# The y_gm projection of a hybrid decoder layer in seven block products

## The chip, the cores and the metric

One core of one Trainium2 chip runs the kernel. The metric is device time in microseconds (us), the median of several executions. TensorE multiplies matrices, VectorE and ScalarE work element by element, GpSimd fills masks and issues accumulating DMAs, and SyncE (SP) issues most of the loads.

## What is computed

One decoder layer on 512 positions and 1024 channels, in float32. A combined input projection feeds a gated MLP (y_gm) and an attention (y_nsa); both are projected, gated and added. The part that matters here:

```python
z = h @ w_in[l]
y_gm = spatial_gating(z_gm, ...)            # gelu(u) * (W_s LN(gelu(v)) + b), 512 x 1024
y_nsa = nsa_attention(z_q, k_cmp, v_cmp, z_ks, z_vs, z_kw, z_vw, sigmoid(z_g))
mix = (mg[:, :, 0] * (y_gm @ w_proj_gm[l]) + mg[:, :, 1] * (y_nsa @ w_proj_nsa[l])) @ w_out[l]
```

`w_proj_gm` is 1024 x 1024, so `y_gm @ w_proj_gm` multiplies a 512x1024 matrix by a 1024x1024 one. w_in, w_proj_nsa, w_out and the two feed-forward matrices (FF1, FF2) are the other large products.

## The kernel before, in words

**Precision.** Each float32 operand is split into a high part (a copy to float32r) and a low part (operand minus high part). A product takes three matmuls into the same PSUM bank: high x high, high x low, low x high (`mm3`, L132). `split` (L142) does this for weights: ScalarE writes `whi` (L150), VectorE subtracts to `wlo` (L151). Both have three buffers.

**The stream of weights.** `Stream` (L41) holds an ordered list of items. Each is one split, cut from a chunk that SP loads into a ring of buffers (L80); the ring `raw` has two buffers of 8 KB a partition. `ws.get()` hands out the next item and writes down the split of the item two places ahead, so that a split waits for the `whi` buffer of the product three before it. A chunk's next load waits for the last split that reads its buffer. The order of instructions on an engine is planned when the kernel is built and isn't always the written one, except under `manual_schedule`.

**The stages**, in the order of TensorE: u (L345 to 407); the v half of z_gm as seven block products (`products` L434, loop L464), with sums of weight blocks on VectorE in place (L223 to 229) in buffers of `rpool`, closed at L483; z_kc and z_vc (L524), each column tile by `dense_a` (L396): 8 steps of k, 3 matmuls of 512 columns each; the compression (L536), whose matmuls are 65 columns wide; z_ks and z_kw (L577), with the spatial gating `sg_mm` between them (L562); vs and vw (L595), whose weights are 256 and 280 columns and whose eight sums fill all eight PSUM banks; the projection of y_gm (L616); z_q (L624); then attention with z_m between its steps, the projection of y_nsa, w_out, FF1 and FF2.

**Around the change.** `sg_mm` writes uT (u times the gate, which is y^T) in eight tiles of 128 channels by 512 positions, and ScalarE and VectorE at once make ygh and ygl of them (L572, L575). After vs and vw the eight banks are emptied into V by ScalarE (L609) and VectorE (L612). The projection then takes for each of 8 tiles of 128 output channels a `whi`, `wlo` pair of 8x128 as stationary operand and ygh, ygl as the moving one, 24 matmuls of 512 columns, and ScalarE copies the bank to Y0 (L620). Its weights are four 1 MB chunks in ring `raw`, each cut into two items (`cols_a(w_pg, 0, 1024)`, L256). `bank()` (L121) takes PSUM banks in a fixed turn. `slab` (L113) takes one of eight 16 KB buffers.

The masks of the attention (Bm, Dc) are filled in `apool`, opened at L485, by GpSimd (L492 to 500), and scaled by ScalarE (L503). They are first read in the scores, after z_q.

The multiplication in seven products is in the kernel already, for v and for three quarters of FF2; there the stationary operand is the activation and the weights move, 512 columns at a time. Its order is `ORDER = (1, 2, 6, 5, 7, 3, 4)` (L177), and products add up in three banks in turn (A: 1, 6, 7, 4; B: 2; C: 5, 3), each emptied between two of them.

Of the kernel before, what the change touches and what calls it, by code (L numbers as in the profile page):

```python
# [16 lines left out]
P = 128  # L17
# [83 lines left out]
def layer_kernel(ctx: ExitStack, tc: tile.TileContext, x, w_in, gm_ln_g, gm_ln_b, gm_w_s, gm_b_s,  # L101
# [11 lines left out]
    def slab(name, shape, dt=F32):  # L113
        return slabs.tile(shape, dt, tag="slab", name=name)
# [39 lines left out]
    def add(shape, dmas, pieces, ring="raw"):  # L154
        c = ws.chunk(ring, shape, dmas)
        for view, dst in pieces:
            ws.item([c], lambda c=c, view=view, dst=dst: split(view(c["tile"]), dst))
# [76 lines left out]
    def s13(d):  # L234
        def go():
            for i in range(2):
                dma_add(d["S"]["tile"][:, i], d["U"]["tile"][:, i])
        return go

    add(**dict(shape=[1, 768], dmas=[(lambda t: t, wv[:, 0:1, 0:768])],  # L240
                       pieces=[((lambda t, j=j: t[:, 0, 384 * j:384 * j + 384]), None) for j in range(2)]))
    add(**dict(shape=[1, 768], dmas=[(lambda t: t, wv[:, 1:2, 0:768])],
# [7 lines left out]
    for k in range(0, 8, 2):  # L250
# [2 lines left out]
            dmas=[(lambda t: t[:, :, 0:256], wv[:, k:k + 2, C_VS:C_VS + 256]),  # L253
                  (lambda t: t[:, :, 256:536], wv[:, k:k + 2, C_VW:C_VW + 280])],
            pieces=[((lambda t, j=j: t[:, j]), None) for j in range(2)]))
    cols_a(w_pg, 0, 1024)  # L256
    cols_a(w_in, C_Q, 1024)
    cols_a(w_in, C_ZM, 2048)
    cols_a(w_pn, 0, 1024)
# [109 lines left out]
    def block(t, i):  # L369
        return t[:, i].rearrange("p (k t) -> p k t", k=4)  # L370
# [93 lines left out]
    for p in ORDER:  # L464
# [16 lines left out]
        if p == 7:  # L481
            cw_load(0, cmp_w1_k)
    early_pool.close()  # L483
    att = ctx.enter_context(ExitStack())
    apool = att.enter_context(tc.tile_pool(name="apool", bufs=1))  # L485
    Kh = apool.tile([P, 2, 1056], F32R, name="Kh")
    Kl = apool.tile([P, 2, 1056], F32R, name="Kl")
    Vch = apool.tile([32, 2, HD], F32R, name="Vch")
    Vcl = apool.tile([32, 2, HD], F32R, name="Vcl")
    Bm = apool.tile([P, 4, 512], F32, name="Bm")  # L490
    Dm = Bm[:, 0]
    nc.gpsimd.iota(Dm, pattern=[[-1, 512]], base=384, channel_multiplier=1,  # L492
                   allow_small_or_imprecise_dtypes=True)
    nc.gpsimd.affine_select(Dm, Dm, pattern=[[-1, 512]], compare_op=ALU.is_ge, fill=BIG,
                            base=384, channel_multiplier=1)
    Dc = apool.tile([P, 4, 32], F32, name="Dc")
    nc.gpsimd.iota(Dc, pattern=[[128, 4], [-16, 32]], base=-15, channel_multiplier=1,
                   allow_small_or_imprecise_dtypes=True)
    nc.vector.tensor_scalar(Dc, Dc, -0.5, None, op0=ALU.add)
    nc.gpsimd.affine_select(Dc, Dc, pattern=[[128, 4], [-16, 32]], compare_op=ALU.is_ge, fill=BIG,  # L500
                            base=-31, channel_multiplier=1)
    for i in (3, 2, 1, 0):
        nc.scalar.activation(Bm[:, i], Dm, AF.Copy, scale=2.0 ** -(i + 1))  # L503

    cw_load(1, cmp_w1_v)

# [49 lines left out]
        nc.vector.tensor_sub(Vcl, pv2, Vch.bitcast(F32))  # L556


    ygh = slab("ygh", [P, 8, S], F32R)
    ygl = slab("ygl", [P, 8, S], F32R)  # L560

    def sg_mm(g):  # L562
        ps = bank()
        for n in range(4):
            nc.tensor.matmul(ps[:, n * P:(n + 1) * P], v[:, n, g * P:(g + 1) * P], WsT[:, g],
                             start=True, stop=True)
        uv = uT[:, g].rearrange("p (n i) -> p n i", n=4)
        tmp = wpool.tile([P, 4, P], F32, tag="tmp", bufs=NTMP, name=f"sg{g}")
        nc.vector.tensor_tensor(tmp, ps.rearrange("p (n i) -> p n i", n=4),
                                bsb[:, g:g + 1].to_broadcast([P, 4, P]), op=ALU.add)  # L570
        nc.vector.tensor_mul(uv, uv, tmp)
        nc.scalar.activation(ygh[:, g], uT[:, g], AF.Copy)  # L572

    def sg_lo(g):
        nc.vector.tensor_sub(ygl[:, g], uT[:, g], ygh[:, g].bitcast(F32))  # L575

    for i in range(4):  # L577
        pc = ws.get()
        ps = bank()
        dense_a(ps, pc, xh, xl)  # L580
        ks = slice(32 + (i // 2) * S, 32 + (i // 2 + 1) * S)
        nc.scalar.activation(Kh[:, i % 2, ks], ps, AF.Copy)
        nc.vector.tensor_sub(Kl[:, i % 2, ks], ps, Kh[:, i % 2, ks].bitcast(F32))
        if i == 0:
            cmp_out()
        sg_mm(2 * i)
        sg_mm(2 * i + 1)
        sg_lo(2 * i)
        sg_lo(2 * i + 1)


    V = slab("V", [P, 2, 4, S], F32R)
    Vh, Vl = V[:, 0], V[:, 1]
    sb = [bank(t) for t in BANKS]
    for k in range(8):  # L595
        hi, lo = ws.get()
        for t in range(4):
            ts_ = slice(t * P, (t + 1) * P)
            for e in range(2):
                cs = slice(0, 256) if e == 0 else slice(256, 536)  # L600
                ps = sb[2 * t + e][:, 0:cs.stop - cs.start]
                nc.tensor.matmul(ps, xh[:, k, ts_], hi[:, cs], start=k == 0, stop=False)  # L602
                nc.tensor.matmul(ps, xl[:, k, ts_], hi[:, cs], start=False, stop=False)
                nc.tensor.matmul(ps, xh[:, k, ts_], lo[:, cs], start=False, stop=k == 7)  # L604
# [8 lines left out]


    Y0 = slab("Y0", [P, 8, S])
    for c in range(8):  # L616
        pc = ws.get()
        ps = bank()
        dense_a(ps, pc, ygh, ygl)
        nc.scalar.activation(Y0[:, c], ps, AF.Copy)  # L620
    nc.vector.tensor_scalar(E1, E1, 1.0, None, op0=ALU.add)
    Qh = slab("Qh", [P, 8, S], F32R)
    Ql = slab("Ql", [P, 8, S], F32R)
# [389 lines left out]
```

## Time and profile before

| | us |
|---|---|
| median of 3 runs | 891.54 (890.77 to 891.58) |
| profiled execution, its own time | 891.16 |
| span of the profiled execution | 889.4 |
| TensorE busy | 874.5 (98%) |
| VectorE, ScalarE, GpSimd busy | 529.6, 384.6, 24.3 |
| mean granted clock of TensorE | 0.997 |
| moved by DMA | 104.79 MB, 118 GB/s |

PE is TensorE's matmuls, PEld its weight loads, DVE is VectorE, ACT ScalarE, POOL GpSimd, SP SyncE. [...] `[x <-A]` behind a row says that the engine stood idle for x us and what released it. Some matmul records are missing from the trace.

### The profile page before, as it was taken

The numbers are of one execution on the slowest core, as the hardware profiler recorded it, in microseconds if no ns is written. First come the engines' busy times: TensorE is split into PE (matmuls) and PEld (weight loads), VectorE is DVE, ScalarE is ACT, GpSimd is POOL, SyncE is SP. The second block draws the span as 40 slices with busy tenths as digits, with TensorE's granted clock in tenths as the row PEclk, the third lists the DMA queues.
The fourth block names the chain that finished last, engine by engine and source line by source line (L and its number), as shares of the span: only waits on it lengthen the run. The fifth ranks groups of instructions, "written<-read, shape, count | busy, mean of one in ns | idle before, by whom it ended". The sixth has DMA issues, their size and how long they took to land.

```text
span 889.4 us, 11012 instructions
## 1 busy us (share of the span) xinstructions
PE 874.5 (98%) x4264; PEld 729.9 (82%) x4264; DVE 529.6 (60%) x1005; ACT 384.6 (43%) x668; POOL 24.3 (3%) x36
## 2 busy tenths in 40 slices
PE   8999999999999999999999999999999999999995
PEld 6888798988888888788878888888888888888884
DVE  3595935542236776666745588457457635853467
ACT  3555413242225656555633412563355345534500
POOL 0000000000000000000000000020011001100000
PEclk9999999999999999999999999999999999999998
DMA  6643810343321111121145441675566747541401
GB/s 200 221 154 95 250 59 25 95 145 95 95 94 49 48 48 48 53 91 48 48 143 188 142 142 48 189 166 173 181 158 127 237 139 168 129 133 47 142 24 71
DMA packets 70773, 104.79 MB, mean 118 GB/s; under 512 B 2432, under 2 KB 50368, under 8 KB 70720
## 3 DMA queue, kind: packets, MB, share of 16 engines
q1 hardware_dynamic: 62752, 83.99, 28.8%
q0 software_dynamic: 3456, 12.58, 7.5%
q10 hardware_dynamic: 4512, 7.50, 2.8%
q8 instruction: 33, 0.54, 0.2%
q14 instruction: 20, 0.16, 0.1%
HBM read 89.39 MB, written 2.10 MB: 103 GB/s over the span
## 4 chain that ended last, share of the span: by engine, by line
PE 96%; DVE 2%; DMA 1%; ACT 1%; issue 0%; SPq 0%; ACTq 0%; DVEq 0%
PE ps L133 19%; PE ps L134 19%; PE ps L135 19%; PE ps L451 5%; PE ps L449 5%; PE ps L452 5%; PE ps L819 3%; PE ps L817 3%; PE ps L818 3%; PE ps L744 2%; PE ps L539 2%; PE ps L759 1%; PE ps L761 1%; PE ps L760 1%; PE ps L602 1%; PE ps L604 1%
## 5 line engine op out<-in xcount | busy, mean ns | idle before, releaser
L151 DVE TENSOR_TENSOR wlo<-raw,whi 128x1024 fp32r<-128x1024 f32 (+3 forms) x116 | 134.0, 1162 | 157.4 <-ACT whi L150 154.0
L150 ACT ACTIVATE whi<-raw 128x1024 fp32r<-128x1024 f32 (+3 forms) x116 | 116.6, 1009 | 196.2 <-PE ps L134 142.7
L133 PE MATMUL ps<-xh,whi 128*128 128x512 f32 x320 | 129.7, 405 | 1.2 <-ACT whi L150 1.2
L134 PE MATMUL ps<-xl,whi 128*128 128x512 f32 x320 | 125.9, 394 | 0.0
L135 PE MATMUL ps<-xh,wlo 128*128 128x512 f32 x320 | 125.7, 393 | 0.0
L134 PE MATMUL ps<-hTl,whi 128*128 128x512 f32 x232 | 90.3, 389 | 0.0
L133 PE MATMUL ps<-hTh,whi 128*128 128x512 f32 x232 | 90.3, 389 | 0.0
L135 PE MATMUL ps<-hTh,wlo 128*128 128x512 f32 x232 | 90.3, 389 | 0.0
L135 PEld LDWEIGHTS ps<-xh,wlo 128*128 128x128 f32 x320 | 60.5, 189 | 13.1
L133 PEld LDWEIGHTS ps<-xh,whi 128*128 128x128 f32 x320 | 60.8, 190 | 11.5 <-ACT whi L150 2.0
L134 PEld LDWEIGHTS ps<-xl,whi 128*128 128x128 f32 x320 | 60.7, 190 | 9.9 <-DVE xl L343 0.4
L449 PE MATMUL ps<-whi,y 128*128 128x512 f32 x168 | 65.5, 390 | 0.0
L451 PE MATMUL ps<-whi,y 128*128 128x512 f32 x168 | 65.5, 390 | 0.0
L452 PE MATMUL ps<-wlo,y 128*128 128x512 f32 x168 | 65.5, 390 | 0.0
L703 ACT ACTIVATE PP<-PP,nm 128x512 f32<-128x512 f32 (+3 forms) x64 | 35.7, 559 | 35.6 <-DVE nm L697 35.3
L133 PEld LDWEIGHTS ps<-hTh,whi 128*128 128x128 f32 x232 | 43.6, 188 | 9.1
L135 PEld LDWEIGHTS ps<-hTh,wlo 128*128 128x128 f32 x232 | 43.6, 188 | 9.0
L134 PEld LDWEIGHTS ps<-hTl,whi 128*128 128x128 f32 x232 | 43.6, 188 | 8.9
L150 ACT ACTIVATE whi<-S 128x1024 fp32r<-128x1024 f32 x24 | 25.6, 1065 | 48.4 <-PE ps L451 35.3
L151 DVE TENSOR_TENSOR wlo<-S,whi 128x1024 fp32r<-128x1024 f32 x24 | 29.4, 1225 | 25.1 <-ACT whi L150 25.1
L909 DVE TENSOR_TENSOR y<-RR,y 128x512 fp32r<-128x512 f32 x50 | 33.1, 688 | 16.0 <-ACT y L908 16.0
L449 PEld LDWEIGHTS ps<-whi,y 128*128 128x128 f32 x168 | 31.5, 188 | 6.7
(235 smaller groups left out, 1712.6 us busy)
## 6 DMA issues: line engine op xcount, KB each, us to landing
raw<-in_w_in_dram SPq DMA_DIRECT2D x17, 1024.0 KB, 5.3
raw<-in_w_ff_dram SPq DMA_DIRECT2D x14, 1024.0 KB, 5.4
raw<-in_w_ff_dram SPq DMA_DIRECT2D x12, 512.0 KB, 4.2
S<-in_w_ff_dram SPq DMA_DIRECT2D x12, 512.0 KB, 4.1
S<-raw POOLq DMA_DIRECT2D x12, 512.0 KB, 6.7
S<-in_w_ff_dram SPq DMA_DIRECT2D x6, 1024.0 KB, 5.5
raw<-in_w_proj_gm_dram SPq DMA_DIRECT2D x4, 1024.0 KB, 5.0
raw<-in_w_proj_nsa_dram SPq DMA_DIRECT2D x4, 1024.0 KB, 4.9
```

The costliest lines, as they stand in the source:

```text
L133: nc.tensor.matmul(ps, hi, mh, start=start, stop=False)
L134: nc.tensor.matmul(ps, hi, ml, start=False, stop=False)
L135: nc.tensor.matmul(ps, lo, mh, start=False, stop=stop)
L150: nc.scalar.activation(hi, r, AF.Copy)
L151: nc.vector.tensor_sub(lo, r, hi.bitcast(F32))
L449: nc.tensor.matmul(ps, yh, hi[:, kk], start=opens and h == 0 and kk == 0, stop=False, skip_group_check=True)
L451: nc.tensor.matmul(ps, yl, hi[:, kk], start=False, stop=False, skip_group_check=True)
L452: nc.tensor.matmul(ps, yh, lo[:, kk], start=False, stop=h == 1 and kk == 1, skip_group_check=True)
L703: nc.scalar.activation(t, t, AF.Exp, bias=nm[:, e, i:i + 1], scale=-1.0, accum_out=sm[:, e, i:i + 1])
L817: nc.tensor.matmul(ps, th, hi[:, cs], start=start, stop=False)
L818: nc.tensor.matmul(ps, tl, hi[:, cs], start=False, stop=False)
L909: nc.vector.tensor_sub(Y[c][1][:, rows], t, Y[c][0][:, rows].bitcast(F32))
```

## The change

The projection of y_gm is done as two halves of the output channels (n = 0, 1). For each, the 1024x512 weights and the 1024x512 y^T are seen as 2x2 blocks, and seven products of sums of blocks take the place of eight. A block of weights is 512x256, one of y^T 512 channels by 256 positions. One product is one item of the stream: 2 tiles of output channels x 4 steps of k x 3 matmuls of 256 columns, with the weights stationary.

The weights of a half come as two chunks: two blocks in ring `raw`, two in a new ring `W` with one buffer in a new pool `mpool`. The sums are made by VectorE in place, but for one in a tile `s3`. The blocks of y^T take the place of ygh and ygl: eleven steps (seven splits, four sums in uT), two written down after each `ws.get()` of vs and vw, into slabs y12, y56, y37 and y4. A product's bank is copied to its quarter of Y0 by ScalarE (1, 6, 5, 4) or added to it or subtracted from it by VectorE (2, 3, 7). `mpool` closes after the projection, and `apool`, with the masks, opens only then; what was needed earlier of it (Kh, Kl, Vch, Vcl) moves to `kpool`.

```diff
@@ -237,6 +237,37 @@
                 dma_add(d["S"]["tile"][:, i], d["U"]["tile"][:, i])
         return go
+    ws.ring("W", 1, lambda shape, n: res["mpool"].tile([P] + shape, F32, tag="W", bufs=1, name=n),
+            ready=lambda: "mpool" in res)
+    def du_here(src, c0):
+        def blk(n, k):
+            return src[:, 4 * k:4 * k + 4, c0 + 256 * n:c0 + 256 * n + 256]
+        one, two = (lambda t: t[:, 0]), (lambda t: t[:, 1])
+        cu = ws.chunk("raw", [2, 4, 256], [(two, blk(0, 0)), (one, blk(1, 1))])
+        cw = ws.chunk("W", [2, 4, 256], [(one, blk(0, 1)), (two, blk(1, 0))])
+        d = {}
+        def item(p):
+            def make():
+                (a22, a11), (a12, a21) = (c["tile"].rearrange("p a k c -> a p k c") for c in (cu, cw))
+                out = split({1: a11, 2: a12, 6: a11, 5: a21, 7: d.get("s3"), 3: a12, 4: a22}[p])
+                if p == 1:
+                    d["s3"] = res["mpool"].tile([P, 4, 256], F32, tag="T", bufs=1, name=f"s3_{state['w']}")
+                    nc.vector.tensor_add(d["s3"], a21, a11)
+                    nc.vector.tensor_add(a21, a21, a22)
+                elif p == 2:
+                    nc.vector.tensor_add(a11, a11, a21)
+                elif p == 6:
+                    nc.vector.tensor_add(a12, a12, a11)
+                return out
+            ws.item([cu] if p in (4, 7) else [cu, cw], make)
+        for p in ORDER:
+            item(p)
     add(**dict(shape=[1, 768], dmas=[(lambda t: t, wv[:, 0:1, 0:768])],
                        pieces=[((lambda t, j=j: t[:, 0, 384 * j:384 * j + 384]), None) for j in range(2)]))
     add(**dict(shape=[1, 768], dmas=[(lambda t: t, wv[:, 1:2, 0:768])],
@@ -253,7 +284,9 @@
             dmas=[(lambda t: t[:, :, 0:256], wv[:, k:k + 2, C_VS:C_VS + 256]),
                   (lambda t: t[:, :, 256:536], wv[:, k:k + 2, C_VW:C_VW + 280])],
             pieces=[((lambda t, j=j: t[:, j]), None) for j in range(2)]))
-    cols_a(w_pg, 0, 1024)
+    pgv = w_pg.rearrange("(k p) c -> p k c", p=P)
+    for n in range(2):
+        du_here(pgv, 512 * n)
     cols_a(w_in, C_Q, 1024)
     cols_a(w_in, C_ZM, 2048)
     cols_a(w_pn, 0, 1024)
@@ -482,25 +515,13 @@
             cw_load(0, cmp_w1_k)
     early_pool.close()
     att = ctx.enter_context(ExitStack())
-    apool = att.enter_context(tc.tile_pool(name="apool", bufs=1))
-    Kh = apool.tile([P, 2, 1056], F32R, name="Kh")
-    Kl = apool.tile([P, 2, 1056], F32R, name="Kl")
-    Vch = apool.tile([32, 2, HD], F32R, name="Vch")
-    Vcl = apool.tile([32, 2, HD], F32R, name="Vcl")
-    Bm = apool.tile([P, 4, 512], F32, name="Bm")
-    Dm = Bm[:, 0]
-    nc.gpsimd.iota(Dm, pattern=[[-1, 512]], base=384, channel_multiplier=1,
-                   allow_small_or_imprecise_dtypes=True)
-    nc.gpsimd.affine_select(Dm, Dm, pattern=[[-1, 512]], compare_op=ALU.is_ge, fill=BIG,
-                            base=384, channel_multiplier=1)
-    Dc = apool.tile([P, 4, 32], F32, name="Dc")
-    nc.gpsimd.iota(Dc, pattern=[[128, 4], [-16, 32]], base=-15, channel_multiplier=1,
-                   allow_small_or_imprecise_dtypes=True)
-    nc.vector.tensor_scalar(Dc, Dc, -0.5, None, op0=ALU.add)
-    nc.gpsimd.affine_select(Dc, Dc, pattern=[[128, 4], [-16, 32]], compare_op=ALU.is_ge, fill=BIG,
-                            base=-31, channel_multiplier=1)
-    for i in (3, 2, 1, 0):
-        nc.scalar.activation(Bm[:, i], Dm, AF.Copy, scale=2.0 ** -(i + 1))
+    kpool = att.enter_context(tc.tile_pool(name="kpool", bufs=1))
+    Kh = kpool.tile([P, 2, 1056], F32R, name="Kh")
+    Kl = kpool.tile([P, 2, 1056], F32R, name="Kl")
+    Vch = kpool.tile([32, 2, HD], F32R, name="Vch")
+    Vcl = kpool.tile([32, 2, HD], F32R, name="Vcl")
+    mid = ctx.enter_context(ExitStack())
+    res["mpool"] = mid.enter_context(tc.tile_pool(name="mpool", bufs=1))
     cw_load(1, cmp_w1_v)
@@ -556,9 +577,6 @@
         nc.vector.tensor_sub(Vcl, pv2, Vch.bitcast(F32))
-    ygh = slab("ygh", [P, 8, S], F32R)
-    ygl = slab("ygl", [P, 8, S], F32R)
     def sg_mm(g):
         ps = bank()
         for n in range(4):
@@ -569,11 +587,6 @@
         nc.vector.tensor_tensor(tmp, ps.rearrange("p (n i) -> p n i", n=4),
                                 bsb[:, g:g + 1].to_broadcast([P, 4, P]), op=ALU.add)
         nc.vector.tensor_mul(uv, uv, tmp)
-        nc.scalar.activation(ygh[:, g], uT[:, g], AF.Copy)
-    def sg_lo(g):
-        nc.vector.tensor_sub(ygl[:, g], uT[:, g], ygh[:, g].bitcast(F32))
     for i in range(4):
         pc = ws.get()
         ps = bank()
@@ -585,15 +598,34 @@
             cmp_out()
         sg_mm(2 * i)
         sg_mm(2 * i + 1)
-        sg_lo(2 * i)
-        sg_lo(2 * i + 1)
     V = slab("V", [P, 2, 4, S], F32R)
     Vh, Vl = V[:, 0], V[:, 1]
+    y12 = slab("y12", [P, 4, D], F32R)
+    y56 = slab("y56", [P, 4, D], F32R)
+    y37 = slab("y37", [P, 4, D], F32R)
+    y4 = slab("y4", [P, 2, D], F32R)
+    Yg = {p: (block(t, i), block(t, i + 1)) for p, (t, i) in
+          {1: (y12, 0), 2: (y12, 2), 5: (y56, 0), 6: (y56, 2), 3: (y37, 0), 7: (y37, 2), 4: (y4, 0)}.items()}
+    b11, b12, b21, b22 = (uT[:, k:k + 4, c:c + 256] for k in (0, 4) for c in (0, 256))
+    def y_split(p, src):
+        nc.scalar.activation(Yg[p][0], src, AF.Copy)
+        nc.vector.tensor_sub(Yg[p][1], src, Yg[p][0].bitcast(F32))
+    steps = [lambda: y_split(1, b11), lambda: y_split(2, b21), lambda: nc.vector.tensor_sub(b11, b11, b12),
+             lambda: y_split(5, b11), lambda: nc.vector.tensor_sub(b12, b22, b12), lambda: y_split(3, b22),
+             lambda: nc.vector.scalar_tensor_tensor(b22, b11, -1.0, b22, op0=ALU.mult, op1=ALU.subtract),
+             lambda: y_split(6, b22), lambda: y_split(7, b12),
+             lambda: nc.vector.scalar_tensor_tensor(b21, b22, -1.0, b21, op0=ALU.mult, op1=ALU.subtract),
+             lambda: y_split(4, b21)]
     sb = [bank(t) for t in BANKS]
     for k in range(8):
         hi, lo = ws.get()
+        for _ in range(2):
+            if steps:
+                steps.pop(0)()
         for t in range(4):
             ts_ = slice(t * P, (t + 1) * P)
             for e in range(2):
@@ -613,11 +645,51 @@
     Y0 = slab("Y0", [P, 8, S])
-    for c in range(8):
-        pc = ws.get()
-        ps = bank()
-        dense_a(ps, pc, ygh, ygl)
-        nc.scalar.activation(Y0[:, c], ps, AF.Copy)
+    for n in range(2):
+        yg = {}
+        for p in ORDER:
+            where = {1: "A", 2: "B", 5: "C", 6: "A", 3: "C", 7: "A", 4: "A"}[p]
+            hi, lo = ws.get()
+            opens = p in (1, 2, 5)
+            if opens:
+                yg[where] = bank()
+            ps = yg[where]
+            for j in range(2):
+                js = slice(j * P, (j + 1) * P)
+                o = ps[:, j * 256:(j + 1) * 256]
+                for k in range(4):
+                    bh, bl = (b[:, k] for b in Yg[p])
+                    nc.tensor.matmul(o, hi[:, k, js], bh, start=opens and j == 0 and k == 0, stop=False,
+                                     skip_group_check=True)
+                    nc.tensor.matmul(o, hi[:, k, js], bl, start=False, stop=False, skip_group_check=True)
+                    nc.tensor.matmul(o, lo[:, k, js], bh, start=False, stop=j == 1 and k == 3,
+                                     skip_group_check=True)
+            c, h = {1: (0, 0), 2: (0, 0), 6: (0, 1), 5: (2, 1), 7: (2, 1), 3: (0, 1), 4: (2, 0)}[p]
+            y0 = Y0[:, 4 * n + c:4 * n + c + 2, 256 * h:256 * h + 256]
+            ps = ps.rearrange("p (k i) -> p k i", k=2)
+            if p in (1, 6):
+                nc.scalar.activation(y0, ps, AF.Copy)
+            elif p in (4, 5):
+                nc.scalar.activation(y0, ps, AF.Copy, scale=-1.0)
+            else:
+                nc.vector.tensor_tensor(y0, y0, ps, op=ALU.subtract if p == 7 else ALU.add)
+    mid.close()
+    apool = att.enter_context(tc.tile_pool(name="apool", bufs=1))
+    Bm = apool.tile([P, 4, 512], F32, name="Bm")
+    Dm = Bm[:, 0]
+    nc.gpsimd.iota(Dm, pattern=[[-1, 512]], base=384, channel_multiplier=1,
+                   allow_small_or_imprecise_dtypes=True)
+    nc.gpsimd.affine_select(Dm, Dm, pattern=[[-1, 512]], compare_op=ALU.is_ge, fill=BIG,
+                            base=384, channel_multiplier=1)
+    Dc = apool.tile([P, 4, 32], F32, name="Dc")
+    nc.gpsimd.iota(Dc, pattern=[[128, 4], [-16, 32]], base=-15, channel_multiplier=1,
+                   allow_small_or_imprecise_dtypes=True)
+    nc.vector.tensor_scalar(Dc, Dc, -0.5, None, op0=ALU.add)
+    nc.gpsimd.affine_select(Dc, Dc, pattern=[[128, 4], [-16, 32]], compare_op=ALU.is_ge, fill=BIG,
+                            base=-31, channel_multiplier=1)
+    for i in (3, 2, 1, 0):
+        nc.scalar.activation(Bm[:, i], Dm, AF.Copy, scale=2.0 ** -(i + 1))
     nc.vector.tensor_scalar(E1, E1, 1.0, None, op0=ALU.add)
     Qh = slab("Qh", [P, 8, S], F32R)
     Ql = slab("Ql", [P, 8, S], F32R)
```

## Rows read from the trace of the kernel before

**Rows 1.** the page: busy time and share by engine, and the chain by engine

```profile
PE 874.5 (98%) x4264; PEld 729.9 (82%) x4264; DVE 529.6 (60%) x1005; ACT 384.6 (43%) x668; POOL 24.3 (3%) x36
...
PE 96%; DVE 2%; DMA 1%; ACT 1%; issue 0%; SPq 0%; ACTq 0%; DVEq 0%
```

**Rows 2.** waits of PE, whole span: us in total, times, longest us

```profile
PE ps L133 <- ACT whi L150: 1.2, 2, 1.0
...
PE ps L602 <- DVE sg L569: 0.2, 1, 0.2
```

**Rows 3.** stretches: us, busy PE, PEld, DVE, ACT, POOL, PEclk, DMA share, GB/s

```profile
162.70:187.10 24.40, 24.22 (x195) 23.92 (x194) 10.48 (x15) 8.34 (x12) 0.00 (x0) 1.00 0.36 110
187.10:230.70 43.60, 43.60 (x195) 36.08 (x194) 12.34 (x16) 13.91 (x27) 0.00 (x0) 1.00 0.34 109
230.70:274.30 43.60, 43.60 (x194) 36.12 (x193) 14.01 (x15) 12.44 (x17) 0.00 (x0) 1.00 0.31 98
```

**Rows 4.** PE in order of time, projection of y_gm: start us, us, operation

```profile
187.13 0.40 PE L133 MATMUL ps<-ygh,whi 128*128 128x512 f32 x1
...
225.25 0.39 PE L133 MATMUL ps<-ygh,whi 128*128 128x512 f32 x1
...
230.69 0.39 PE L133 MATMUL ps<-xh,whi 128*128 128x512 f32 x1
```

**Rows 5.** PE in order of time, compression and FF1; loads of vs, vw

```profile
118.37 14.67 PE L539 MATMUL ps<-misc,cw 128*128 128x65 f32 x128
...
L604 PEld LDWEIGHTS ps<-wlo,xh x64: 187/188/192, 162.9 to 186.9; 128*128 128x128 f32 x64
...
556.16 0.28 PE L133 MATMUL ps<-hTh,e 128*128 128x256 f32 x1
...
558.50 0.28 PE L135 MATMUL ps<-hTh,e 128*128 128x256 f32 x1
```

**Rows 6.** groups by line and shape (busy us, mean ns); then VectorE in time

```profile
L151 DVE TENSOR_TENSOR wlo<-raw,whi 128x1024 fp32r<-128x1024 f32 x99 | 120.6, 1225 | 140.4 <-ACT whi L150 137.2 <-DMA raw<-in_w_ff_dram 3.2
L150 ACT ACTIVATE whi<-raw 128x1024 fp32r<-128x1024 f32 x99 | 104.5, 1059 | 179.8 <-PE ps L134 139.3 <-PE ps L451 14.4 <-PE ps L818 6.6
...
L575 DVE TENSOR_TENSOR ygl<-uT,ygh 128x512 fp32r<-128x512 f32 x8 | 5.5, 687 | 2.1 <-ACT ygh L572 2.1
...
L572 ACT ACTIVATE ygh<-uT 128x512 fp32r<-128x512 f32 x8 | 5.0, 631 | 13.6 <-DVE uT L571 13.6
...
L224 DVE TENSOR_TENSOR s<-s,raw x2: 1220/1220/1221, 44.8 to 53.9; 128x1024 f32<-128x1024 f32 x2
...
106.30 2.35 DVE L151 TENSOR_TENSOR wlo<-raw,whi 128x1024 fp32r<-128x1024 f32 x2
```

**Rows 7.** stretch in the v projection, columns as in rows 3

```profile
44.00:54.00 10.00, 10.00 (x46) 8.29 (x45) 10.00 (x10) 6.69 (x9) 0.00 (x0) 1.00 0.78 269
```

**Rows 8.** VectorE in order of time, last steps of uT and first V eviction

```profile
151.19 0.68 DVE L571 TENSOR_TENSOR uT<-uT,sg 128x512 f32<-128x512 f32 x1
...
166.03 0.69 DVE L571 TENSOR_TENSOR uT<-uT,sg 128x512 f32<-128x512 f32 x1
...
186.46 0.42 DVE L612 TENSOR_TENSOR V<-ps,V 128x256 fp32r<-128x256 f32 x1
```

**Rows 9.** VectorE in order of time, end of the v projection

```profile
85.70 0.29 DVE L517 COPY misc<-ps 128x32 f32<-128x32 f32 x2 [2.14 <-PE ps L516]
```

**Rows 10.** POOL, SP and PE in order of time, start of the z_kc projection

```profile
87.19 0.56 POOL L492 IOTA Bm<- 128x512 f32 x1 [28.75 <-DVE wlo L151]
...
89.63 1.50 SPq L80 DMA_DIRECT2D raw<-in_w_in_dram  x2
...
95.97 0.50 PE L133 MATMUL ps<-xh,whi 128*128 128x512 f32 x1 [0.99 <-ACT whi L150]
```

**Rows 11.** DMA issues: count, KB each, median us to landing; then SP's min/median/max

```profile
raw<-in_w_proj_gm_dram SPq DMA_DIRECT2D x4, 1024.0 KB, 5.0
...
DMA to landing us min/median/max: 2.7/5.0/10.9
```

## What the change is predicted to do

> **What bounds the kernel now.** I read the page first: TensorE is busy for 98% of the span, and the chain that ended last is 96% TensorE [rows 1]. The waits of TensorE come next: in the whole span it waits for about 5 us, of which the change can touch only 1.2 us at the start of the z_kc projection and 0.2 us at the start of vs and vw [rows 2]. So time is won here only by taking work from TensorE, and lost by anything that makes it wait. Then the stretches: vs and vw take 24.4 us and the projection of y_gm 43.6 us, both at a granted clock of 1.00, with VectorE busy for 10.5 and 12.3 us and ScalarE for 8.3 and 13.9 us of them [rows 3]. There is room beside TensorE, but in vs and vw the change fills it. Last, the matmuls in order of time. A row's duration (0.39 us) overlaps its neighbours, so I take the distance of starts: 225.25 to 230.69 holds the 24 matmuls of one column tile, 5.44 us, or 0.2267 us for 512 columns; the stage runs from 187.13 to 230.69, 43.56 us [rows 4].
>
> **TensorE's part.** Removed: 8 tiles x 8 k x 3 = 192 matmuls of 512 columns, 43.56 us. Added: 2 halves x 7 products x 2 x 4 x 3 = 336 of 256 columns. The same shape (weights stationary, 256 columns of activations moving) stands in the first FF1 tiles: 556.16 to 558.50 holds 20 starts, 0.117 us each [rows 5]. That is more than half of 0.2267, so seven eighths of the arithmetic isn't seven eighths of the time: 336 x 0.117 = 39.3 us. Bounds: 0.115 from the compression's matmuls of 65 columns, which I take as the floor for a weight load and its matmul (14.67 us / 128), gives 38.6; 0.127 from vs and vw (24.4 us / 192, half of them 280 columns wide and a small wait included) gives 42.7 [rows 3, 5]. I take 0.118, a little over FF1 for the 14 changes of product: 39.7 us, a gain of 3.9 (0.9 to 5.0). One product is then 24 x 0.118 = 2.8 us.
>
> [...] The row first: a weight load is recorded at 188 ns, and the change has 144 more of them [rows 5]. [...] By that measure the new stage would hold 336 x 188 ns = 63.2 us of loads. The trace disagrees with reading it as a limit: 192 loads at 188 ns, 36 us, fit in the 24.4 us of vs and vw. It is a rival below.
>
> **Splits and sums of the weights.** 8 splits become 14, with the same 128x1024 tiles: ScalarE 1.06 us and VectorE 1.23 us each, 1.14 back to back [rows 6]. Eight in-place sums on VectorE cost 1.22 us each, from the sums of the v projection [rows 6]. Eight evictions on ScalarE become eight there and six on VectorE, which at this width (128x512) cost 0.63 and 0.69 us [rows 6]. For one half: VectorE 7 x 1.14 + 4 x 1.14 + 3 x 0.69 = 14.6 us, ScalarE 7 x 1.06 + 4 x 0.63 = 9.9 us, under 7 x 2.8 = 19.7 us of TensorE. The v projection is the nearest case: half-products of 12 x 0.227 = 2.7 us with one split each and the same sums, VectorE busy for all of 44 to 54, and TensorE never stopped [rows 7]. I cost this at nothing as long as it runs in that rhythm: a split starts when the product three before it ends, since `whi` has three buffers, and has 5.6 us.
>
> **Blocks of y^T beside vs and vw.** Removed: eight ScalarE copies and eight VectorE subtractions of ygh and ygl (0.63 and 0.69 [rows 6]). Added: seven copies of 1.06 us, and seven subtractions and four sums, 11 x 1.14 = 12.5 us on VectorE. Its budget from 162.7 to 187.1 is 24.4 us. It now holds 10.5 [rows 3], less two ygl subtractions 1.3, plus 12.5, plus the first three sums of weights 3.4, makes 25.1: 0.7 too much. Three of the eleven steps (products 1 and 5) need only the upper half of uT, which is ready at 151.9, and could run earlier, which leaves 21.7. What waits for VectorE is the first product: its bank is free when the first V eviction has been read, and that ends at 186.88 now, 0.25 us before TensorE needs it at 187.13 [rows 8]. Bounds: everything placed in gaps, no stall; everything in written order, after the last step of uT (166.03 + 0.69 [rows 8], less the 0.6 of a ygl subtraction ahead of it, 166.1) the 11 steps and five splits of 0.65 us reach 181.8, with up to three waits of 1.06 us for ScalarE's copies 185.0, then two splits and three sums 5.7 us, then the eviction 0.42: 187.9 to 191.1, a stall of 0.8 to 4.0 us. Written order isn't kept strictly: the copy of L517, written after the v products, ran at 85.70, ten us before the matmul at 95.97 that follows them [rows 9, 10]. I take 0.6 us.
>
> **Loads.** The first load of ring W (1 MB) can start when the v projection's buffers are released, at 87.1, where GpSimd's iota of the same space starts now [rows 10]. The z_kc weights are issued at 89.63, and TensorE waits 0.99 us for their first split, until 95.97 [rows 10]. If W goes first on SP's queue, its 1 MB takes 5.0 us to land [rows 11], of which 2.5 are a head start: up to 2.5 us more wait; behind z_kc's, nothing. I take 0.1. The second load of W has one buffer to go to: it waits on SP for the split of product 3 of the first half; behind it stand z_q's loads, which wait for later splits anyway, and on VectorE the two sums of the second half wait for it. With the end of product 6 as zero, that split is done at 2.8, the load (5.0 us in the projection's rows [rows 11]) lands at about 8.0, the two sums end at 10.9 with an eviction among them, the split of the next product 2 at 12.4 at the latest, and TensorE wants it at 14.0; product 6 of the second half is ready at 15.9 of 16.8. Slack 0.9 us: I take 0.1, bounds 0 to 1. The two raw slots come free at the same splits of vs and vw as before, and the second chunk is now wanted 20 us later.
>
> **Bias masks.** Iotas, selects and four copies of 0.63 us leave the time from 87.19 on [rows 10] and go behind the projection, beside z_q, where ScalarE is busy for 12.4 of 43.6 us [rows 3]. The scores need them 40 us later. On GpSimd nothing is queued behind them; on ScalarE splits with over 5 us to spare are. Nothing, unless that cover went: then 2.5 us.
>
> **Sum.** -3.9 + 0.6 + 0.1 + 0.1 = -3.1 us against the profiled execution's 891.16 us (span 889.4): 888.1. The median, 891.54, lies 0.4 above that: 888.4.
>
> **Rivals.**
> 1. W's first load ahead of z_kc's. For: its space is free 2.5 us before theirs [rows 10]. Against: it is written later. 1 to 2.5 us: 889.3 to 890.8, taken as 890.0.
> 2. V's eviction held behind the y blocks, in written order. For: 25.1 us of work in 24.4. Against: rows 9. A stall of 2 to 4 us instead of 0.6: 889.8 to 891.8, taken as 891.
> 3. Slower: the sums of the second half are queued on VectorE ahead of product 4's split, and wait there for W's second load. The split then ends at landing + 3.5, and is wanted at 8.4. At 8.0 the stall is 3.1 and the gain is gone; slower by over 0.2% from a landing at 9.8 on, and the slowest load of the trace took 10.9 us where the middle one took 5.0 [rows 11]. A landing at 10.4, with a stall of 5.5, gives 893.9. Against: the split's inputs are there first.
> 4. Loads set the pace: 63.2 us instead of 39.7 gives 911; a pace of 43.56 / 336 = 0.1296 us gives no change, 891.5. Against: rows 5 for both.
>
> **How the numbers follow.** Forecast 0.65 (887.2 to 889.6), rival 1 0.11, rival 2 0.12, rival 3 0.06, rival 4 0.06 (0.01 of it at 911). A run of three tells about 0.2%, 1.8 us, from nothing: faster is under 889.76. Faster: 0.65 + 0.05 of rival 1 + 0.02 of rival 2 = 0.72. Slower: 0.05 of rival 3, 0.01 of rival 4 and 0.01 of rival 2 = 0.07. Same: 0.21. The range goes from 887.0 (0.117 and no stall would be 887.3) to 891.0, which leaves out half of rival 2, rivals 3 and 4 and a little of rival 1, 0.2 together.
>
> **What would show it.** TensorE's 336 starts 0.117 to 0.118 us apart, stage 39.7 us; VectorE nearly full from 163 to 187; a wait of TensorE for an eviction of V or a split at the first product; the wait before 95.97 unchanged; none in the middle. Wrong would be a distance over 0.12 us, a wait over 2 us at 187, or any repeated wait for `whi` or `wlo` in the products.

## Result: the products gained 3.2 us, and the start of z_kc lost more

| | before | after |
|---|---|---|
| median, us | 891.46 (890.77 to 891.58, 4 runs) | 897.30 (896.13 to 898.37, 4 runs) |
| profiled execution, its own time | 891.16 | 898.11 |
| its span | 889.4 | 896.4 |
| mean granted clock of TensorE | 0.997 | 0.990 |

After takes 1.0064 times as long as before (95% interval 1.0052 to 1.0076): 5.8 us slower by the medians (7.0 in the two profiled executions), where 888.4 was predicted and 891.0 was the upper end of the range.

The page of after, busy time by engine, the granted clock in 40 slices, and the chain (the lines of rows 1):

```profile
PE 873.7 (97%) x4408; PEld 735.8 (82%) x4408; DVE 557.7 (62%) x1028; ACT 392.6 (44%) x673; POOL 25.1 (3%) x36
PEclk9999799999999999999999999999999999999998
PE 96%; DVE 2%; DMA 1%; ACT 1%; issue 0%; SPq 0%; DVEq 0%; ACTq 0%
```

The chain is as before and says nothing. The clock line does: the fifth slice, 90 to 112 us, has a 7, a hundred microseconds ahead of the changed projection. The waits of TensorE in after, in us in total, times, and the longest (rows 2 before):

```profile
PE ps L135 <- DVE wlo L151: 6.4, 1, 6.4
PE ps L373 <- DMA xn<-in_x_dram: 2.4, 2, 2.1
PE ps L133 <- ACT whi L150: 2.1, 2, 1.9
```

The first line is new: one wait of 6.4 us for a low part of weights. The third was 1.2 in all [rows 2]. Neither the products (L662 to 665) nor the first V eviction has a line. TensorE in order of time in after shows where the wait is:

```profile
97.80 0.50 PE L133 MATMUL ps<-xh,whi 128*128 128x512 f32 x1 [1.91 <-ACT whi L150]
...
105.88 0.79 PE L135 MATMUL ps<-xh,wlo 128*128 128x512 f32 x1 [6.40 <-DVE wlo L151]
106.47 0.63 PE L133 MATMUL ps<-xh,whi 128*128 128x512 f32 x1
...
110.31 0.63 PE L133 MATMUL ps<-xh,whi 128*128 128x512 f32 x1
```

It is the start of z_kc, the place of rival 1. From 106.47 to 110.31 the starts are 0.427 us apart (nine steps), where a matmul of 512 columns took 0.2267 [rows 4]. The wait, the stretch behind it and the two stages around the change as windows of after (us, busy PE, PEld, DVE, ACT, POOL, granted clock, DMA share, GB/s; rows 3 before):

```profile
97.80:105.88 8.08, 1.47 (x4) 0.60 (x5) 7.73 (x18) 1.96 (x2) 0.00 (x0) 0.68 1.00 279
105.88:110.70 4.82, 4.82 (x11) 3.80 (x12) 4.82 (x6) 0.00 (x0) 0.00 (x0) 0.50 0.52 158
173.50:197.50 24.00, 24.00 (x195) 23.90 (x195) 21.92 (x25) 11.93 (x15) 0.00 (x0) 1.00 0.35 112
197.50:237.80 40.30, 40.30 (x338) 40.30 (x337) 29.54 (x34) 22.20 (x36) 1.65 (x4) 1.00 0.25 79
```

The granted clock is 0.50 from 105.88 to 110.70, after a stretch in which TensorE had run four matmuls in 8 us. The mean of 0.68 over that stretch says that it fell during the wait already: it is 1.00 from 97.80 to 99.50, 0.88 from 99.50 to 101.00 and 0.50 from there to 105.88. In the two stages of the change it is 1.00.

Now the time by starts of stages, before to after, from the matmuls in order of time:

| | before | after | shift |
|---|---|---|---|
| first matmul of z_kc | 95.97 [rows 10] | 97.80 | +1.8 |
| first matmul of the compression | 118.37 [rows 5] | 129.22 | +10.8 |
| first matmul of the projection of y_gm | 187.13 [rows 4] | 197.53 | +10.4 |
| first matmul of z_q | 230.69 [rows 4] | 237.85 | +7.2 |
| end of the span | 889.4 | 896.4 | +7.0 |

Of the +1.8, 0.9 is the longer wait for `whi` (1.91 for 0.99), and most of the rest is the wait for `xn` at the very start (2.4 here, 1.6 in before), which the change doesn't touch. Between z_kc and the compression 9.0 are lost: 6.4 are the wait, 2.4 the half clock behind it (ten starts 0.427 apart instead of 0.227, and one at each end that is longer by 0.4 together), and 0.2 come in because the wait is counted from the end of the last matmul's record, 0.40 us behind its start, where the next could have started 0.227 behind it. From the compression to the projection after is 0.4 shorter, of which 0.2 is the wait for `sg` that is gone [rows 2]. The projection gives 3.2 back, 40.32 us for 43.56.

Who kept the low part? SP of after in order of time (start us, us, operation):

```profile
88.05 0.92 SPq L80 DMA_DIRECT2D W<-in_w_proj_gm_dram  x2
90.38 16.98 SPq L80 DMA_DIRECT2D raw<-in_w_in_dram  x3
```

ScalarE of after in order of time:

```profile
96.69 2.00 ACT L150 ACTIVATE whi<-raw 128x1024 fp32r<-128x1024 f32 x2 [0.28 <-ACT v L508]
```

VectorE of after in order of time:

```profile
97.25 0.21 DVE L549 BATCH_NORM_AGGREGATE mv<-st 128x2 f32<-128x12 f32 x1
...
99.75 1.54 DVE L529 TENSOR_SCALAR v<-v,mv,rs 128x1024 f32<-128x1024 f32 x2
101.20 2.35 DVE L531 TENSOR_TENSOR v<-v,gmc 128x1024 f32<-128x1024 f32 x2
103.47 1.22 DVE L532 TENSOR_TENSOR v<-v,gmc 128x1024 f32<-128x1024 f32 x1
104.61 3.49 DVE L151 TENSOR_TENSOR wlo<-raw,whi 128x1024 fp32r<-128x1024 f32 x3
```

The high part that `wlo` needs was written from 96.69 on and took about 1 us. VectorE didn't stand idle: from 97.25 it ran the end of v's layer norm (aggregate, twelve small steps of the reciprocal root, five steps that normalise v), and only at 104.61 the three subtractions of z_kc, back to back. In before the order was the other way round. VectorE of before:

```profile
95.95 2.36 DVE L151 TENSOR_TENSOR wlo<-raw,whi 128x1024 fp32r<-128x1024 f32 x2 [0.24 <-ACT whi L150]
...
101.45 1.53 DVE L508 TENSOR_SCALAR v<-v,mv,rs 128x1024 f32<-128x1024 f32 x2
```

Nothing of the layer norm was edited. The diff moves two things near this place: the first load of ring W, now on SP ahead of z_kc's weights (88.05 and 90.38), and the masks, which left it. `wlo` had its operands for over 6 us and still ran behind the normalisation. That VectorE ran the order of the built program there is argued from this, not shown by the trace; e2 below, where the program ties the layer norm behind z_kc's first splits, has the first two of them at 96.58.

### The profile page after: what moved, and what is told of

Read it like the earlier page. It is cut to its first block, busy times and chain, and to the rows that moved or that the text cites. A ratio compares the mean times of both kernels' runs of the same rounds, so it can differ in the third digit from the quotient of the medians.

```text
span 896.4 us, 11356 instructions
## 1 busy us (share of the span) xinstructions
PE 873.7 (97%) x4408; PEld 735.8 (82%) x4408; DVE 557.7 (62%) x1028; ACT 392.6 (44%) x673; POOL 25.1 (3%) x36
## 4 chain that ended last, share of the span: by engine, by line
PE 96%; DVE 2%; DMA 1%; ACT 1%; issue 0%; SPq 0%; DVEq 0%; ACTq 0%
PE ps L133 18%; PE ps L135 18%; PE ps L134 18%; PE ps L484 6%; PE ps L482 6%; PE ps L485 6%; PE ps L891 3%; PE ps L889 3%; PE ps L890 3%; PE ps L816 2%; PE ps L560 2%; PE ps L665 1%; PE ps L662 1%; PE ps L664 1%; PE ps L831 1%; PE ps L833 1%
## 5 line engine op out<-in xcount | busy, mean ns | idle before, releaser
L151 DVE TENSOR_TENSOR wlo<-raw,whi 128x1024 fp32r<-128x1024 f32 (+3 forms) x114 | 131.4, 1159 | 130.0 <-ACT whi L150 129.8
L150 ACT ACTIVATE whi<-raw 128x1024 fp32r<-128x1024 f32 (+3 forms) x114 | 114.4, 1008 | 190.9 <-PE ps L134 136.2
L485 PEld LDWEIGHTS ps<-wlo,y 128*128 128x128 f32 x168 | 31.5, 188 | 6.7
```

Source lines behind the costliest of these rows:

```text
L150: nc.scalar.activation(hi, r, AF.Copy)
L151: nc.vector.tensor_sub(lo, r, hi.bitcast(F32))
L485: nc.tensor.matmul(ps, yh, lo[:, kk], start=False, stop=h == 1 and kk == 1, skip_group_check=True)
```

## The experiments

Theory A: W's load, put ahead of z_kc's, delays these a little, and the order planned with that delay in it puts the layer norm of v ahead of z_kc's splits on VectorE; that order and the half clock behind it cost most, the load itself about 1 us. Theory B: the load itself, 1 MB ahead of z_kc's on the DMA engines, costs it all. Theory C: the masks that left the place changed the order. (Each expectation below states its own theories by letter; what it calls B isn't always this B.) In the edits, `tc.issue_after(x)` puts what stands in its block behind instruction x on its engine.

**e1_load_behind: W's first load behind z_kc's on SP.**

```diff
                 for dv, src in c["dmas"]:
-                    self.nc.sync.dma_start(dv(c["tile"]), src)
+                    with self.behind() if c["ring"] == "W" and c["n"] == 0 else ExitStack():
+                        i = self.nc.sync.dma_start(dv(c["tile"]), src)
+                if c["ring"] == "raw":
+                    self.last_raw = i
...
+    ws.behind = lambda: tc.issue_after(ws.last_raw.ins)
```

> The changed kernel, with the first load of ring W queued on SP behind the second load of the z_kc weights; nothing else is edited, and VectorE's planned order at the start of z_kc is then again that of the kernel before. Theory A (the load in front delays the z_kc weights, and the plan made with that delay puts the normalisation of v ahead of their splits on VectorE): the wait of 6.4 us and the half clock go, the wait before z_kc is 1 us again, and the gain of the products remains: 887.5 to 888.5 us. Theory B (the seven products and the y blocks cost the time somewhere else, and the stall at z_kc only moves it): 893 us or more.

Measured: 887.69 us (886.24 to 888.62), 0.9958 of before (0.9943 to 0.9973). SP of e1 in order of time:

```profile
91.23 9.02 SPq L81 DMA_DIRECT2D raw<-in_w_in_dram  x3
100.35 4.94 SPq L81 DMA_DIRECT2D W<-in_w_proj_gm_dram  x2
...
199.28 0.92 SPq L81 DMA_DIRECT2D W<-in_w_proj_gm_dram  x2
```

VectorE of e1 in order of time:

```profile
97.50 2.36 DVE L155 TENSOR_TENSOR wlo<-raw,whi 128x1024 fp32r<-128x1024 f32 x2
```

TensorE of e1 in order of time, first matmuls of z_kc, of the projection and of z_q:

```profile
97.52 0.50 PE L136 MATMUL ps<-xh,whi 128*128 128x512 f32 x1 [0.78 <-ACT whi L154]
...
188.22 0.28 PE L666 MATMUL ps<-y,whi 128*128 128x256 f32 x1
...
228.53 0.40 PE L136 MATMUL ps<-xh,whi 128*128 128x512 f32 x1
```

With the load behind, the first two splits are ahead of the layer norm again, the 6.4 us wait is gone, and the change is worth 3.8 us where 3.1 were predicted, at 887.69 for 888.4. The projection takes 228.53 - 188.22 = 40.31 us. This kernel is faster than before (by 0.4%) and than after. C falls: the masks have moved here too.

**e2_dve_order: W's load left in front, the layer norm put behind z_kc's first splits.**

```diff
-            for t in range(4):
-                nc.vector.bn_aggr(mv[:, t], st6[:, t])
-            rstd(mv[:, :, 1], EPS, 0, 4)
+            with tc.issue_after(los[-2].ins):
+                for t in range(4):
+                    nc.vector.bn_aggr(mv[:, t], st6[:, t])
+                rstd(mv[:, :, 1], EPS, 0, 4)
```

> The changed kernel with the first load of ring W still in front of the z_kc weights, but with the statistics and the normalisation of v tied on VectorE behind the splits of the first z_kc chunk. Theory A (most of the loss is VectorE's order, 6.4 us of wait and about 2.6 us of half clock, the late load itself only some 1 us): 888 to 890 us, with a wait of about 2 us left before the first z_kc matmul. Theory B (the load itself holds TensorE up, whatever VectorE's order): the stall stays near 6 us and the time near 897 us.

Measured: 889.63 us (888.50 to 891.28), 0.9983 of before (0.9973 to 0.9992). The waits of TensorE in e2:

```profile
PE ps L133 <- ACT whi L152: 1.9, 1, 1.9
...
PE ps L135 <- DVE wlo L153: 0.5, 1, 0.5
```

VectorE of e2 in order of time:

```profile
96.58 2.36 DVE L153 TENSOR_TENSOR wlo<-raw,whi 128x1024 fp32r<-128x1024 f32 x2 [0.56 <-ACT whi L152]
```

A window of e2 over the place (columns as above):

```profile
94.00:112.00 18.00, 15.56 (x68) 12.34 (x67) 16.63 (x31) 6.76 (x9) 0.00 (x0) 1.00 0.98 293
```

The load is still 2.3 us ahead of z_kc's on SP (86.85 and 89.17), and 7.7 of after's 897.30 us are gone. The wait for `whi` is the same 1.9 us, the one for `wlo` is 0.5, and the clock stays at 1.00. B falls: in front, the load costs about 889.63 - 887.69 = 1.9 us, as rival 1 had it (1 to 2.5), and the order on VectorE the rest. The 1.9 is not the load's alone, since e2 also puts z_kc's third split ahead of the layer norm, which before and e1 don't.

**e3_load_only and e4_masks_only: before, with one part of the change each.** e4 takes before's masks to the place after the projection, Kh, Kl, Vch and Vcl to `kpool`. e3 does that and adds the load, into a buffer that nothing reads:

```diff
+    ws.ring("W", 1, lambda shape, n: res["mpool"].tile([P] + shape, F32, tag="W", bufs=1, name=n),
+            ready=lambda: "mpool" in res)
+    ws.chunk("W", [2, 4, 256], [((lambda t: t[:, 0]), pgv[:, 0:4, 256:512]), ((lambda t: t[:, 1]), pgv[:, 4:8, 0:256])])
```

> The kernel before with its eight tiles of y_gm, with the masks moved behind the projection and with the first load of ring W added, which nothing reads. Theory A: the same stall at z_kc as in the changed kernel without the products' gain of 3.2 us: 900 to 901.5 us. Rival (the products, the sums or the y blocks are needed for the loss): 891 to 893 us.

> The kernel before with the masks moved behind the projection of y_gm and the small pool for K and V opened in their place; no load is added. Theory A: VectorE's order at z_kc is as before, no stall: 891 to 892 us. Rival (the moved masks change the order there): 897 us or more.

Measured: e3 901.72 us (901.22 to 902.57), 1.0119 of before (1.0102 to 1.0136); e4 890.82 (890.20 to 891.63), 0.9992 (0.9983 to 1.0002). TensorE's wait in e3:

```profile
PE ps L135 <- DVE wlo L151: 6.9, 1, 6.9
```

z_kc's splits on VectorE of e3:

```profile
104.50 3.49 DVE L151 TENSOR_TENSOR wlo<-raw,whi 128x1024 fp32r<-128x1024 f32 x3
```

And in e4:

```profile
PE ps L133 <- ACT whi L150: 1.4, 2, 1.1
```

A load that nothing reads makes the kernel of before 10.2 us slower (901.72 against 891.49 for before, measured beside it), with the wait of after and the splits at 104.50 as in after; the masks alone change nothing that can be told. Two DMA instructions on SP are enough for the whole loss. That the planner moved the layer norm because it counted with later weights is argued from this, not shown: its reckoning isn't in a trace.

**e5_second_load_late: the second load of W a product later (from here on all kernels are e1 with an edit).**

```diff
-            ws.item([cu] if p in (4, 7) else [cu, cw], make)
+            ws.item([cu] if p == 7 else [cu, cw], make)
```

> As e1_load_behind (887.69 us), but product 4 of the first half also holds ring W's chunk, so the second load of W can start only behind product 4's split instead of product 3's, one product (24 x 0.120 = 2.9 us) later. The result is computed in full. Theory as in the prediction (the second load has 0.9 us of slack before VectorE's sums hold up the products): the first wait of TensorE appears in the second half, about 2 us, and the time is about 889.7. Rival (the slack is larger than computed, because the load or the sums come sooner than the working has them): no wait of TensorE in the products, 887.7 within 0.6.

Measured: 887.73 us (887.37 to 888.76). This is the rival's time, but it tells nothing of the slack, because the edit didn't move the load. VectorE of e5, the split of product 3 in the first half:

```profile
196.69 1.23 DVE L155 TENSOR_TENSOR wlo<-W,whi 128x1024 fp32r<-128x1024 f32 x1 [1.65 <-ACT whi L154]
```

SP of e5, the second load of W:

```profile
197.94 0.92 SPq L81 DMA_DIRECT2D W<-in_w_proj_gm_dram  x2
```

The load goes out 1.25 us after the split of product 3 begins, when that has been read. e9 does what e5 was to do.

**e9_second_load_behind: the second load behind z_q's first on SP.** As e5, and:

```diff
-                    with self.behind() if c["ring"] == "W" and c["n"] == 0 else ExitStack():
+                    with self.behind() if c["ring"] == "W" else ExitStack():
```

> As e1_load_behind, but the second load of W stands on SP behind the first load of z_q, which waits for the split of product 4 of the first half: so it is issued one product (2.9 us) later and shares the DMA engines with another 1 MB. (e5_second_load_late was meant to do that, but its load was still issued right behind product 3's split, 1.25 us after that split began, as in e1_load_behind.) The result is computed in full. Theory (about 1 us of slack, as in the prediction; in e1_load_behind the split of product 2 ends 1.0 us before its product is due): the delay of 3 to 5 us leaves a wait of TensorE of 2 to 4 us at product 2 or 6 of the second half, and some half clock behind it, 890 to 893 us. Rival (the order on VectorE gives way and hides it): a wait under 0.5 us, 887.7 to 888.3.

Measured: 893.29 us (891.21 to 894.79), 1.0019 of before (1.0009 to 1.0029): 5.6 us more than e1. TensorE of e9 in order of time, from the first matmul of the projection to the first of z_q:

```profile
187.59 0.28 PE L666 MATMUL ps<-y,whi 128*128 128x256 f32 x1
...
211.41 0.39 PE L669 MATMUL ps<-y,wlo 128*128 128x256 f32 x1 [0.39 <-DVE wlo L155]
...
216.21 0.39 PE L666 MATMUL ps<-y,whi 128*128 128x256 f32 x1 [1.91 <-ACT whi L154]
...
217.16 0.58 PE L666 MATMUL ps<-y,whi 128*128 128x256 f32 x1 [0.45 <-ACT whi L154]
...
234.48 0.40 PE L136 MATMUL ps<-xh,whi 128*128 128x512 f32 x1
```

SP of e9, the second load of W:

```profile
201.94 1.13 SPq L81 DMA_DIRECT2D W<-in_w_proj_gm_dram  x2
```

A window of e9 behind the waits:

```profile
217.16:223.65 6.49, 6.49 (x28) 6.22 (x29) 2.99 (x3) 1.73 (x2) 0.00 (x0) 0.50 0.01 3
```

VectorE of e9, the split of product 2 in the second half:

```profile
210.13 1.23 DVE L155 TENSOR_TENSOR wlo<-W,whi 128x1024 fp32r<-128x1024 f32 x1 [4.38 <-ACT whi L154]
```

VectorE of e1, the split of product 6 in the second half:

```profile
212.41 1.23 DVE L155 TENSOR_TENSOR wlo<-raw,whi 128x1024 fp32r<-128x1024 f32 x1
```

The load goes out 201.94 - 187.59 = 14.35 us behind the start of the projection, where in e1 it is 199.28 - 188.22 = 11.06: 3.3 us later. TensorE waits 0.4 us in product 2 and 2.4 us in product 6 of the second half, and runs at 0.50 behind that. So the slack was smaller than the delay. Its size is read from e1: there the split of product 6 ends at 212.41 + 1.23 = 213.64 and its product is due at 188.22 + 9 x 2.88 = 214.14, so it is 0.5 us, for the 0.9 of the prediction. e9 can't give it, because VectorE's order changed there too: the split of product 2 stands ahead of the first two sums, where in e1 it stands behind them (208.87, the sums at 205.99 and 207.73).

**e6_y_lows_twice: 8 us more of VectorE beside vs and vw.**

```diff
-        nc.vector.tensor_sub(Yg[p][1], src, Yg[p][0].bitcast(F32))
+        for _ in range(2):
+            nc.vector.tensor_sub(Yg[p][1], src, Yg[p][0].bitcast(F32))
```

> As e1_load_behind (887.69 us), but each of the seven subtractions that make the low parts of the y blocks is done twice, which adds 7 x 1.14 = 8 us of VectorE beside vs and vw. The result is the same. Theory as in the prediction (VectorE is nearly full there, 21.7 to 25.1 us of work in 24.4): TensorE waits 5 to 8 us around the first product of the projection, 893 to 896. Rival (the work has room that the working doesn't count, in gaps before vs and vw or behind the first product): a wait under 1.5 us, under 889.2.

Measured: 892.98 us (892.05 to 895.75), 1.002 of before (1.0009 to 1.003): 5.3 more than e1. TensorE of e6 in order of time, the first product:

```profile
192.24 0.58 PE L667 MATMUL ps<-y,whi 128*128 128x256 f32 x1 [3.51 <-DVE V L649]
192.61 0.41 PE L669 MATMUL ps<-y,whi 128*128 128x256 f32 x1
...
193.89 0.41 PE L669 MATMUL ps<-y,whi 128*128 128x256 f32 x1
...
235.06 0.40 PE L136 MATMUL ps<-xh,whi 128*128 128x512 f32 x1
```

The last row is the first of z_q. A window of e6 behind the wait:

```profile
192.24:197.52 5.28, 5.28 (x24) 5.28 (x25) 4.53 (x9) 0.76 (x1) 0.00 (x0) 0.50 0.00 0
```

The bottleneck is where the prediction put it, V's eviction behind the y blocks. But 8 us more make a wait of 3.5, so by this difference the change had 4.5 us of room there (some of it before vs and vw, where the first y steps run), where the prediction had between -0.7 and 2.7. The wait was under the 5 to 8 us expected; the time came out just under the 893 to 896, since the half clock behind the wait adds to it.

**e7_moving_from_x: the products' moving operand from another place.**

```diff
-                    bh, bl = (b[:, k] for b in Yg[p])
+                    bh, bl = xh[:, k, 0:256], xl[:, k, 0:256]
```

> As e1_load_behind, but the products take their moving operand from xh and xl (positions 0 to 256 of channel tiles 0 to 3) instead of the seven y blocks, so y_gm @ w_proj_gm is left out of the result; the y blocks are still made, and all matmuls have the same shape and count. It asks why starts are 0.120 us apart in the products and 0.117 in FF1, whose moving operand is also a slice of 256 of 512 positions. If the distance comes from where the moving operand lies: 0.117 us, and the stage is 336 x 0.003 = 1.0 us shorter. If it comes from the matmul itself (weights, bank, order of the three): 0.120 again, and the stage keeps its 40.3 us.

Measured: 887.85 us, one run. TensorE in order of time in e7, seven starts 0.120 us apart:

```profile
200.34 0.28 PE L666 MATMUL ps<-xh,whi 128*128 128x256 f32 x1
...
201.06 0.28 PE L666 MATMUL ps<-xh,whi 128*128 128x256 f32 x1
```

The distance doesn't come from where the moving operand lies: a slice of xh, cut as FF1's is, gives 0.120 too.

**e8_stats_behind: z_kc's raw buffer free sooner.** The statistics of the v block from product 7 go behind v's last splits on VectorE:

```diff
+            if p == 7:
+                late.append((st6[:, t, e], vs_))
...
+        if p == 3:
+            with tc.issue_after(los[-1].ins):
+                for o, i in late:
+                    nc.vector.bn_stats(o, i)
```

> As e1_load_behind (887.69 us), but the statistics of the v block that product 7 makes are put behind the last splits of v on VectorE, which frees the raw buffer that z_kc's first weights wait for about 1.2 us sooner. The result is the same. Theory (the wait of about 0.8 us that is left before z_kc's first matmul is a late buffer): the load is issued about 1 us sooner, the wait is gone, and the time is about 886.8. Rival (the wait is set by the load or by ScalarE's split, or the statistics then hold up what follows): 887.7 or more.

Measured: 886.80 us (885.92 to 887.83), 0.9943 of before (0.993 to 0.9957). The wait of TensorE for `whi` there:

```profile
PE ps L136 <- ACT whi L156: 0.6, 2, 0.4
```

The longest wait fell from 0.8 to 0.4 us, half of what was expected; the times of e8 and e1 overlap, so that it is faster than e1 isn't shown. Both are faster than before and than after.

## Why the prediction was wrong, step by step

**Loads, first load of W: the step that failed.** It took 0.1 us, on the ground that the load is written later than z_kc's. It went first, 2.3 us ahead of it on SP. The evidence was on the table: its space came free at 87.1 and z_kc's at 89.63 [rows 10], and the prediction itself had found an instruction run ten us ahead of its written place [rows 9]; it used that row in favour of the change (y steps that can run early) and not against it.

**Rival 1: right place, a fifth of the price.** It priced the load as 1 MB in front of another, 1 to 2.5 us, and e2 measures 1.9. What it left out is that an added load is an input to the order of every engine near it. VectorE had 7.4 us of layer norm that could stand before or behind the first `wlo` (97.25 to 104.61); in before it stood behind, in after before it: 6.4 us of waiting. And the wait costs more than its length: TensorE's granted clock fell to 0.50 in it and stayed there for 4.8 us behind it, so that the 6.4 us cost 9.0. 0.9 + 9.0 = 9.9 us by the trace of after; e3 measures 10.2 for the load by itself, and e1 gets 9.6 back.

**TensorE's part: the mechanism right, the term a little off.** 0.120 us a start for the 0.118 taken, so 40.3 us for 39.7 and a gain of 3.2 for 3.9, inside its bounds. The size fits rows 4: half of the distance at half clock, plus 0.013. With 512 columns that is 0.427 / 2 + 0.013 = 0.2267 [rows 4], with 256 columns 0.2133 / 2 + 0.013 = 0.120 (0.2133 is (193.89 - 192.61) / 6 in e6). FF1's 0.117 [rows 5], on which the term was sized, is the exception; why isn't settled, and e7 rules out the place of the operand. A nearer row stood in vs and vw of before, the stage just ahead of the projection:

```profile
186.38 0.28 PE L602 MATMUL ps<-whi,xh 128*128 128x256 f32 x1
...
186.74 0.29 PE L602 MATMUL ps<-whi,xh 128*128 128x280 f32 x1
```

Three matmuls of 256 columns lie between these two starts, 0.120 us each. Taken from there the term would have been 40.3 us.

**The cost of 144 more weight loads:** not the 63.2 us of rival 4 (336 x 188 ns [rows 5]), as the prediction held: the stage takes 40.3. That they cost nothing isn't shown. PEld is busy for all of the 40.30 us, and every matmul here has its own load, so whether the 0.013 us beyond the columns belongs to the matmul or to its load can't be told; 144 x 0.013 = 1.9 us of the stage come from having 336 of them for 192.

**Splits and sums:** nothing, confirmed; no wait in the products.

**y blocks beside vs and vw:** 0.6 taken, 0 measured, with VectorE busy for 21.9 of 24.0 us, the prediction's 21.7 (three steps run earlier, as it said they could). e6 found 4.5 us of room.

**Second load of W:** 0.1 taken, 0 measured; slack 0.5 instead of 0.9 us (e1). The load took 6.7 us there, from 199.28 to the first sum at 205.99, for the 5.0 of the prediction. Rival 3's place is the neighbour of this one, and e9 shows its price: 5.6 us for a load 3.3 us later.

**Masks:** nothing, confirmed by e4.

**The sum.** With the first load behind, the total comes out near the forecast, -3.2 + 0 against -3.1, and 887.69 measured for 888.4. That is in part luck: the products gave 0.7 less than was taken, and the 0.8 of stalls didn't come. Of the 3.8 us between e1 and before, 3.2 are the products; the other 0.6 aren't accounted for in full (the wait of 0.2 for `sg` is gone). The range was too short above because rival 1 ended at 890.8: it left the plan of VectorE as it was.

## What to carry to other kernels

Where a planner orders the instructions, an added load is not only bytes: ask what the engines near the place where its buffer comes free could run instead, and look in the built order whether they now do. If the load isn't wanted soon, tie it behind the urgent one; here that was worth 9.6 us. And price a wait of TensorE of some microseconds with the half clock that can follow it. Read within one trace each, 6.4 us cost 9.0 in after; in e9 2.8 us cost 6.6 (the projection takes 234.48 - 187.59 = 46.89 us for e1's 40.31); in e6 3.5 us cost 6.0 (the wait, and 235.06 - 192.24 = 42.82 us for 40.31). By the medians e9 and e6 lose 5.6 and 5.3.

## What the runs showed of the hardware that was not expected

With a weight load for each matmul, the distance of two matmuls at a granted clock of 1.00 was half of that at 0.50 plus 0.013 us, with 256 columns as with 512: 0.120 (e7) and 0.2267 [rows 4] against 0.2133 (e6) and 0.427 (after). At 0.50 the two measured distances are in proportion to the columns. It isn't a rule for every width or stage: the compression's matmuls of 65 columns take 0.115 [rows 5], and FF1's of 256 take 0.117 [rows 5].

Behind the waits of 6.4 us (after), 3.5 us (e6) and 2.4 us (e9, two waits with two matmuls between them) TensorE's granted clock was 0.50 for 4.8, 5.3 and 6.5 us. It doesn't always follow: e2 waited 1.9 and 0.5 us and the clock was 1.00 in the whole window, and the fastest of e9's ten executions (891.21 us) had a mean granted clock of 0.997, the profiled one (894.79) 0.992. That a wait of TensorE can bring such a second price, as in these three, is what the prediction's prices of stalls lacked.
